# Linear-memory v and o columns as seven-product pairs ahead of attention, kept in DRAM until their heads

## The chip, the cores and the metric

The kernel runs on one core of one Trainium2 chip. Its time is that of one execution on the device in microseconds (us). A core has TensorE (PE) for matrix products, VectorE (DVE), ScalarE (ACT) and GpSimd (POOL) for the rest, and SyncE (SP), which here only issues DMAs. Each engine works through its own instructions in the order in which the program has them and waits on semaphores for the others. PE writes to PSUM, eight banks of 128 x 512 values; here four belong to a tag "mm" and four to a tag "aux".

## The reference

One inference step of a one-layer hybrid encoder on 512 frames of a new stream ("prompt") and 64 frames of a running one ("sample"), 576 rows in all, model width 1024:

```python
h = layer_norm(ALPHA * x + 0.5 * swiglu_ffn(x, ffn1_w_gu, ffn1_w_down), ln1_g, ln1_b)
z = h @ w_in      # q, k, v, o of 4 memory heads, gates i and f, q, k, v of attention, gates g_m and g_a
h_ml = mlstm(silu(conv(q)), silu(conv(k)) / 16, v, i, f, state)     # linear memory, chunks of 64
y_ml = (norm(h_ml) * ml_norm_g * sigmoid(o)) @ w_ml_proj
y_att = band_attention(qa, ka, va, cache, bias) @ w_att_proj
h = layer_norm(ALPHA * h + (sigmoid(g_m) * y_ml + sigmoid(g_a) * y_att) @ w_out, ln2_g, ln2_b)
y = layer_norm(ALPHA * h + 0.5 * swiglu_ffn(h, ffn2_w_gu, ffn2_w_down), ln3_g, ln3_b)
```

Outputs are y and the new states (convolution rows, memory C, n and m, keys and values). All is float32.

## The kernel before, in words

Activations lie transposed: a tile is 128 features by 576 rows, eight tiles make the width. Every product is computed as three products of rounded parts (float32r): value = hi + lo, and x w becomes hi hi, lo hi and hi lo (`mm3`, L127). **A column** is 128 output features: 8 feature blocks x 3 products x 2 halves of the rows (256 and 320) = 48 matmuls into two "mm" banks (`gemm`, L266). Its weights come as one DMA of 512 KB on SP; `pump` (L187) has ACT round them to hi, and lo is made either by DVE or (for most columns of `w_in`) by ACT, which writes -hi, and a DMA on POOL's queue that adds the raw weights to it (`add_lo`, L174). `plan` (L339 to L367) is the list of all weights in the order of use; `take` and `done` move along it.

**Seven-product pairs.** In both FFNs a gate column and an up column are computed together by a Strassen-like scheme: `Units` (L679) views the pair as a 2 x 2 block product over the two halves of the features and the two halves of the rows (288 each) and needs 7 instead of 8 block products: 7 x 4 feature blocks x 3 = 84 matmuls of 288 rows against 96 of a plain pair. The price is sums: of weights, per pair, on DVE and ACT (`prep`), and of activations, once, in `Combos` (L644): `add` makes 16 sums of halves on DVE, `make`, at high priority, has ACT round each of eight sums of 128 x 576 to hi and write -hi for lo (16 copies), and POOL issues eight DMAs that add the sum to lo. A pair's results are copied out of PSUM by ACT and combined on DVE.

**Stages**, in PE's order, with their starts in the profiled execution: FFN1 (0), the norm LN1 inside a wave of the first attention columns v, k, q and the memory gates "if" (401.5; `WAVE_M`, L1203: half 1 of v, k, q, half 1 of "if", then half 2 of them), attention for column pairs j = 0 to 7 (428.6), gate columns 64 to 71 (about 650), the attention projection "ap" (703), the four memory heads (755, 812.4, 881.6, 950.8), gate columns 56 to 63 (1020), the memory projection "mp" (1083.3), "o" (1134), LN2 and FFN2 (1187), LN3.

**A head** (L1324 to L1527) has eight columns: k, k, q, q, o, o, v, v. k and q go through a convolution (`conv_rest`), v is turned to rows (`turn5`) and split, o goes through a sigmoid and POOL multiplies it by the norm's gain. Between the columns stand the memory's own small products: `weights`, `state`, `hidden`, the norm, and `back`, which turns the normed rows back and multiplies by o.

**What sets the order.** PE's order is written by hand: `Order` (L42) has a modelled clock that every matmul moves on, `later(dt, fn)` puts a piece of work on a heap to be issued once the modelled clock reaches its due time, `od.bg` holds background work with a period, and `gemm` looks at both between matmuls. The other engines' orders are made by the framework's scheduler from issue order and priorities (`hot(n)`: that much higher). Buffers rotate in pools; an instruction that writes a buffer waits until its last reader is done.

In attention the sample rows' values (`values_s`, L1184) multiply probabilities with cached and new values: 2 heads x 3 key blocks (128, 128 and 64 keys) x 3 products, each 64 stationary columns (one head's width) by 64 rows.

Of the kernel before, what the change touches and what calls it, by code (L numbers as in the profile page):

```python
# [81 lines left out]
def tile_layer(ctx: ExitStack, tc: tile.TileContext, ins, outs):  # L82
# [10 lines left out]
    psum = ctx.enter_context(tc.tile_pool(name="psum", bufs=4, space=PSUM))  # L93

# [14 lines left out]
    def slot(dt, pool=None, tag="s", **kw):  # L109
        return (pool or slots).tile([P, T], dt, tag=tag, name=nm(tag), **kw)  # L110

# [54 lines left out]
    EARLY = [("gu2", j, e) for j in range(2) for e in range(2)]  # L166
    CP = (6, 7)
# [10 lines left out]
    def early(pool, key):  # L178
# [3 lines left out]
        hi, lo = parts[c] = tuple(pool.tile([P, 1024], F32R, tag=t, name=nm(t), bufs=len(EARLY)) for t in ("eh", "el"))  # L182
        act(hi, raw)
        add_lo(lo, hi, plan[c][1])

    @hot(30)
    def pump(limit=2):  # L187
        while True:
            c = wst["conv"]
            if wst["dma"] < len(plan) and plan[wst["dma"]][0] in EARLY:  # L190
                wst["dma"] += 1
                continue
            if c < len(plan) and plan[c][0] in EARLY:
                assert c in parts
                wst["conv"] += 1
                continue
# [45 lines left out]
    def done(c):  # L242
        del parts[c]
        wst["used"] -= plan[c][0] not in EARLY
        later(50, pump)
# [433 lines left out]
    class Units:  # L679
# [3 lines left out]
        def __init__(self, n, j0, hr, pool, wp, combos):  # L683
            self.w, self.hr, self.pool, self.wp, self.x = ins[f"w_gu{n}"], hr, pool, wp, combos
            self.raw, self.ws, self.p = {}, {}, {}
            self.js = list(range(j0, FT))

        def load(self, j):
            if j >= FT:
                return  # L690
            w = self.raw[j] = self.wp.tile([P, 2048], F32, tag="wu", name=nm("wu"), bufs=2)
            SP.dma_start(w[:, 0:1024], self.w[j])  # L692
            SP.dma_start(w[:, 1024:2048], self.w[FT + j])
# [11 lines left out]
        @hot(30)  # L705
        def prep(self, j, what):
            if j >= FT:
# [34 lines left out]
        def begin(self, j, tag="mm"):  # L742
            u = dict(j=j, X=bank(tag)[:, :HT_], h=self.hr.tile([P, T], F32, tag="h", name=nm("h"), bufs=FT + 1), tag=tag)
            self.product(u["X"], j, "a11", "b11", True, False)
            self.copy(u["h"][:, :HT_], u["X"])
            return u

        def second(self, u):
            h = u["h"][:, :HT_]
            Y = bank(u["tag"])[:, :HT_]  # L750
            self.product(Y, u["j"], "a12", "b21", True, True)
            with tc.high_priority(offset=60):
                tt(h, Y, h, ALU.add)
                act(h, h, AF.Silu)

        def run(self, tail):
            cur = ahead = None
            for j in self.js + [None]:
# [7 lines left out]
                if j == FT - 1:  # L766
# [10 lines left out]
                self.copy(new["h"][:, HT_:], new["X"])  # L777
# [4 lines left out]
                c = new["c"] = self.pool.tile([P, HT_], F32, tag="c22", name=nm("c22"), bufs=1)  # L782
# [4 lines left out]
                if j == FT - 1:  # L787
# [5 lines left out]
        def finish(self, u):  # L793
            j, h = u["j"], u["h"]
            self.product(u["X"], j, "a22", "t4", False, True)
            with tc.high_priority(offset=60):
                stt(h[:, :HT_], u["X"], -1.0, h[:, :HT_], ALU.mult, ALU.mult)
# [3 lines left out]
            with tc.high_priority(offset=60):  # L801
                tt(h[:, HT_:], u["Z"], h[:, HT_:], ALU.add)
                act(h[:, HT_:], h[:, HT_:], AF.Silu)
                last = tt(h[:, HT_:], h[:, HT_:], u["c"], ALU.mult)
            self.hr_done(j, h, last)
# [26 lines left out]
    def ffn(xs, n, gi, raw, final=None, prev=None):  # L832
        hh = {}
        with tc.tile_pool(name=nm("hr"), bufs=FT, side="right", reuse_waits="tile") as hr, \
# [30 lines left out]
            with tc.tile_pool(name=nm("sw"), bufs=1, side="right", reuse_waits="tile") as sw, \  # L865
                    tc.tile_pool(name=nm("sx"), bufs=1, side="right", reuse_waits="tile") as sx:
                combos.pool = sx
                un = Units(n, CL[n], hr, sx, sw, combos)
# [35 lines left out]
            with tc.tile_pool(name=nm("h1"), bufs=n1, side="right", reuse_waits="tile") as h1, \  # L904
# [3 lines left out]
                ln = Norm(xs, 2.0 * ALPHA, 4.0 * EPS, gi, final)  # L908
# [189 lines left out]
    def att_core(j, st):  # L1098
# [103 lines left out]

    gemm([[(("in", 48), KT)], [(("in", 40), KT)], [(("in", 32), KT)], [("if", KT)]], H,  # L1203
         [out_cb(vf0, "v", 0), out_cb(kf0, "k", 0), lambda hf, ps: act(hs(qf0, hf), ps), gate_cb], WAVE_M)
    ln1.close()
    opool.append(ostack.enter_context(tc.tile_pool(name="op", bufs=8, reuse_waits="tile")))
# [39 lines left out]
    matt = sg  # L1246
    for j in range(KT):
        gemm(one(("ap", j)), OS,
             [lambda hf, ps, m=matt[j]: tt(hs(m, hf), hs(m, hf), ps, ALU.mult)])
# [5 lines left out]
    sgp = gstack.enter_context(tc.tile_pool(name="sg0", bufs=2, side="right", reuse_waits="tile"))  # L1255
# [36 lines left out]
    def conv_rest(R, ct, scale, tail=None):  # L1292
# [7 lines left out]
        hi, lo = slot(F32R, mp, "qk", bufs=8), slot(F32R, mp, "qk", bufs=8)  # L1300
# [23 lines left out]
    def ml_qkov(h, early):  # L1324

        st = {"k": [], "q": [], "og": []}
# [3 lines left out]
        for e in range(2):  # L1330
# [3 lines left out]
            kf, hi, lo = conv_rest(R, ct, 1.0 / 16)  # L1334
# [9 lines left out]
            later(10000, lambda kf=kf, s=k_sink: turn5(kf, s))  # L1344
        qtail = mp.tile([P, 2, NS], F32, tag="qtail", name=nm("qtail"))
        for e in range(2):
# [3 lines left out]
            _, hi, lo = conv_rest(R, ct, 1.0, qtail[:, e, :])  # L1350
            st["q"].append((hi, lo))
        st["qtail"] = qtail
        early(st)
        for e in range(2):
            o = slot(F32, hp, "og")
            st["og"].append(o)
            gemm(one(("in", 24 + 2 * h + e)), H, [lambda hf, ps, o=o: act(hs(o, hf), ps, AF.Sigmoid)])
            ts(o, o, ccol(C_NG + 2 * h + e), 0.0, ALU.mult, ALU.add, eng=POOL)
        for e in range(2):
            vf = slot(F32, mp, "qf", bufs=2)  # L1360
            gemm(one(("in", 16 + 2 * h + e)), H, [lambda hf, ps, vf=vf: act(hs(vf, hf), ps)])
# [6 lines left out]
            later(2500, lambda vf=vf, s=v_sink: turn5(vf, s))  # L1368
        return st

    def ml_early(h, st):

        st["W"] = W = []
# [53 lines left out]
        for b in range(5):  # L1427
            later(15440 + 3120 * b, lambda b=b: weights(b))

    def ml_late(h, st):  # L1430
# [59 lines left out]
        def back(e):  # L1490
# [5 lines left out]
            og = st["og"][e]  # L1496
            tt(og[:, :NP_], pt, og[:, :NP_], ALU.mult)
            tt(og[:, NP_:], pt2[:, :NS], og[:, NP_:], ALU.mult)
# [7 lines left out]
        t = 4500  # L1506
        for e in range(2):
            later(t, lambda e=e: state(e))
            t += 1800
        for b in range(5):  # L1510
            later(t, lambda b=b: hidden(b))
            t += 1700
        later(t + 2500, norm)

    for h in range(4):
        st = ml_qkov(h, lambda st, h=h: ml_early(h, st))
        ml_late(h, st)
# [3 lines left out]
    for j in range(2):  # L1521
        s = sg[j] = slot(F32, sgp, "sg")
        gemm(one(("in", 56 + j)), H, [lambda hf, ps, s=s: act(hs(s, hf), ps, AF.Sigmoid)])
    od.drain()
# [6 lines left out]
    gmp = hts.enter_context(tc.tile_pool(name="gm", bufs=6, reuse_waits="tile"))  # L1531
# [10 lines left out]
    for j in range(2, KT):  # L1542
        s = sg[j] = slot(F32, gmp, "sg")
        gemm(one(("in", 56 + j)), H, [lambda hf, ps, s=s: act(hs(s, hf), ps, AF.Sigmoid)])
# [23 lines left out]
    for i, key in enumerate(EARLY):  # L1568
        later(4000 + 6800 * i, lambda key=key: early(epool, key))
# [96 lines left out]
```

## Time and profile before

| | us |
|---|---|
| median of three executions | 1597.05 (1596.64 to 1605.06) |
| the profiled execution | 1601.19 |
| its span, first to last instruction | 1599.4 |
| PE busy | 1580.9 |
| DVE busy | 990.2 |
| ACT busy | 875.1 |
| POOL busy | 199.9 |

The span is what the trace covers; 1.8 us of the profiled execution lie outside it. Times in a row of the profile count from the span's start. In a row of a timeline stand start, length, engine, line, operation, what is written and read, shapes and count, and in brackets how long the engine idled before it and which instruction ended that. L123 is the line of the helper that issues matmuls, L133 that of transposes, L137 of ACT's copies, L140, L143 and L147 of DVE's and POOL's operations, so rows are told apart by the tiles they name. PE's ends are modelled, so where paces are needed differences of starts are used.

### The profile page before, as it was taken

The numbers are of one execution on the slowest core, as the hardware profiler recorded it, in microseconds if no ns is written. First come the engines' busy times: TensorE is split into PE (matmuls) and PEld (weight loads), VectorE is DVE, ScalarE is ACT, GpSimd is POOL, SyncE is SP. The second block draws the span as 40 slices with busy tenths as digits, with TensorE's granted clock in tenths as the row PEclk, the third lists the DMA queues.
The fourth block names the chain that finished last, engine by engine and source line by source line (L and its number), as shares of the span: only waits on it lengthen the run. The fifth ranks groups of instructions, "written<-read, shape, count | busy, mean of one in ns | idle before, by whom it ended". The sixth has DMA issues, their size and how long they took to land. (4 is left out here: it accounts for less than half of the span.)

```text
span 1599.4 us, 29416 instructions
## 1 busy us (share of the span) xinstructions
PE 1580.9 (99%) x11851; PEld 1559.0 (97%) x11851; DVE 990.2 (62%) x2041; ACT 875.1 (55%) x1587; POOL 199.9 (12%) x363
## 2 busy tenths in 40 slices
PE   9999999999999999999999999999999999999998
PEld 8999999999999999999999999999999999999997
DVE  7777777636777677551545637234686777776636
ACT  7554556314677677863758576642446455555223
POOL 2000000000424334011212111102111000000000
PEclk9999999999999999999999999999999999999999
DMA  9222222224466666577656564642435232213333
GB/s 264 95 105 81 106 80 74 83 86 130 135 163 154 154 148 151 113 168 169 145 138 137 127 149 104 156 109 83 129 106 139 80 106 81 105 54 97 112 94 121
DMA packets 65921, 193.18 MB, mean 121 GB/s; under 512 B 7288, under 2 KB 17144, under 8 KB 65784
## 3 DMA queue, kind: packets, MB, share of 16 engines
q1 hardware_dynamic: 51672, 145.16, 27.3%
q0 software_dynamic: 13536, 45.62, 16.9%
q8 instruction: 93, 1.52, 0.4%
q10 hardware_dynamic: 576, 0.52, 0.1%
q14 instruction: 44, 0.36, 0.1%
HBM read 177.31 MB, written 9.24 MB: 117 GB/s over the span
## 5 line engine op out<-in xcount | busy, mean ns | idle before, releaser
L123 PE MATMUL mm<-s,wh 128*128 128x288 f32 (+2 forms) x3856 | 786.6, 298 | 0.9 <-ACT h L137 0.4
L123 PEld LDWEIGHTS mm<-s,wh 128*128 128x128 f32 x3856 | 618.8, 189 | 5.5 <-ACT s L418 0.9
L123 PE MATMUL mm<-s,wl 128*128 128x288 f32 (+2 forms) x1912 | 565.0, 295 | 0.8 <-DVE wl L140 0.7
L123 PEld LDWEIGHTS mm<-s,wl 128*128 128x128 f32 x1912 | 360.8, 189 | 1.2 <-DVE wl L140 1.2
L137 ACT ACTIVATE wh<-wr 128x1024 fp32r<-128x1024 f32 (+2 forms) x163 | 164.9, 1014 | 272.6 <-PE mm L123 246.4
L140 DVE TENSOR_TENSOR wl<-wr,wh 128x1024 fp32r<-128x1024 f32 (+2 forms) x88 | 101.2, 1157 | 128.0 <-ACT wh L137 127.8
L123 PE MATMUL mm<-h,wh 128*128 128x256 f32 (+1 forms) x672 | 134.7, 294 | 0.0
L140 DVE TENSOR_TENSOR wl<-ws,wh 128x1024 fp32r<-128x1024 f32 x39 | 47.8, 1225 | 104.0 <-ACT wh L137 103.8
L123 PEld LDWEIGHTS mm<-h,wh 128*128 128x128 f32 x672 | 107.6, 188 | 0.2
L123 PE MATMUL mm<-h,wl 128*128 128x256 f32 (+1 forms) x336 | 98.7, 294 | 0.0
L441 POOL TENSOR_TENSOR rs<-var,mhalf 128x2 f32<-128x2 f32 (+1 forms) x6 | 5.2, 863 | 740.2 <-DVE var L143 384.0
L137 ACT ACTIVATE wh<-ws 128x1024 fp32r<-128x1024 f32 x39 | 41.4, 1061 | 94.8 <-PE mm L123 94.3
L123 PE MATMUL mm<-tx,wh 128*128 128x288 f32 x448 | 92.4, 298 | 0.0
L176 POOL DMA_DIRECT2D wl<-in_w_in x66 | 57.9, 878 | 244.6 <-ACT wl L137 176.2
L137 ACT ACTIVATE wl<-wh 128x1024 fp32r<-128x1024 f32 x74 | 78.0, 1054 | 0.5
L123 PEld LDWEIGHTS mm<-tx,wh 128*128 128x128 f32 x448 | 72.1, 189 | 0.0
L123 PE MATMUL mm<-tx,wl 128*128 128x288 f32 x224 | 66.1, 295 | 0.0
L123 PEld LDWEIGHTS mm<-h,wl 128*128 128x128 f32 x336 | 63.0, 188 | 0.0
L123 PE MATMUL mm<-tx,ah 128*128 128x288 f32 x296 | 62.2, 302 | 0.1
L137 ACT ACTIVATE wh<-wu 128x1024 fp32r<-128x1024 f32 x39 | 41.4, 1062 | 30.6 <-PE mm L123 30.0
L123 PE MATMUL mm<-hb,wh 128*128 128x256 f32 (+1 forms) x280 | 56.5, 294 | 0.0
L123 PE MATMUL mm<-hc,wh 128*128 128x256 f32 (+1 forms) x280 | 56.3, 294 | 0.0
(322 smaller groups left out, 3294.0 us busy)
## 6 DMA issues: line engine op xcount, KB each, us to landing
wu<-in_w_gu SPq DMA_DIRECT2D x78, 512.0 KB, 4.3
wr<-in_w_in SPq DMA_DIRECT2D x72, 512.0 KB, 3.7
wl<-in_w_in POOLq DMA_DIRECT2D x66, 512.0 KB, 5.5
wr<-in_w_dn SPq DMA_DIRECT2D x40, 512.0 KB, 3.5
wr<-in_w_dn SPq DMA_DIRECT2D x20, 384.0 KB, 3.1
G<-in_rbias SPq DMA_DIRECT2D x16, 256.0 KB, 2.7
wr<-in_w_ap SPq DMA_DIRECT2D x8, 512.0 KB, 3.7
wl<-in_w_ap POOLq DMA_DIRECT2D x8, 512.0 KB, 6.1
```

Source lines behind the costliest of these rows:

```text
L123: PE.matmul(out, lhsT, rhs, start=start, stop=stop, **kw)
L137: ACT.activation(out, in_, func, **kw)
L140: return (eng or DVE).tensor_tensor(out, a, b, op=op)
L176: POOL.dma_start(lo, src, accum_op=ALU.add)
L441: return y, POOL.tensor_tensor(y, v, mhalf[:, :n], op=ALU.pow)
```

## The change

1. Columns 16 to 31 (v and o of the four heads) leave the heads. The first v pair (16, 17) is computed plainly behind LN1's wave, with weights loaded early; the other seven pairs, o0, v1, o1, v2, o2, v3, o3, follow as seven-product pairs (`Columns`, a second kind of `Units`), all ahead of attention. The sums of LN1's output come from `Combos`, so LN1 keeps its unsplit output as LN2 did (sixteen more ACT copies).
2. Their results (o after its sigmoid) are stored to DRAM, sixteen tiles of 128 x 576, and loaded again in their head. The gated attention output (eight tiles) is stored behind "ap" and loaded again ahead of "mp".
3. A head computes k, k, q, q and one gate column (56 + h). The norm's gain moves from POOL into the last product of `back`. Due times of the head's pieces change: weights at 11000 + 2600 b (15440 + 3120 b before), state at 5500, hidden at 19500 + 2200 b, the norm at 31000. Gate columns 60 to 62 follow the heads, and column 63 stands alone beside the eight splits of the heads' output (`ht_split`), which stood beside six gate columns.
4. `values_s` takes hi and lo of the values side by side as 128 stationary columns: 12 matmuls instead of 18, and one more ACT copy and two small DVE additions in place of two ACT copies.

In the core of the diff, `Units` takes its sources and its last steps from the subclass (`GateUp` holds the FFN's); that part is left out here.

```diff
@@ plan
     plan.append(("if", ins["w_if"]))
+    plan_in((16, 17))
+    stops.append(len(plan))
     for j in range(1, KT):
         plan_in((48 + j, 40 + j, 32 + j))
     plan_in(range(64, 72))
     plan += [(("ap", j), ins["w_ap"][j]) for j in range(KT)]
     for h in range(4):
-        plan_in((8 + 2 * h, 9 + 2 * h, 2 * h, 2 * h + 1, 24 + 2 * h, 25 + 2 * h, 16 + 2 * h, 17 + 2 * h))
-    plan_in(range(56, 64))
+        plan_in((8 + 2 * h, 9 + 2 * h, 2 * h, 2 * h + 1, 56 + h))
+    plan_in(range(60, 64))
@@ new class
+    class Columns(Units):
+        def __init__(self, pairs, sinks, out, pool, wp, combos):
+            super().__init__([(w_in[a], w_in[b]) for a, b in pairs], 0, pool, wp, combos)
+            self.sinks, self.out = sinks, out
...
+        def done21(self, u):
+            act(u["21"], u["X"], scale=-1.0)
+        def done(self, u):
+            self.sinks[u["j"]](u["o"])
@@ values_s
+            blocks = (P, 5), (P, 6), (NS, 4)
             for e in range(2):
                 r = slice(64 * e, 64 * e + 64)
-                for b, (ks, vb) in enumerate(((P, 5), (P, 6), (NS, 4))):
-                    mm3(po[0:64, r], vc[:ks, vb, e, 0:64], vc[:ks, vb, e, 64:128], th[:ks, b, r], tl[:ks, b, r],
-                        b == 0, b == 2)
+                for b, (ks, vb) in enumerate(blocks):
+                    for x in (th, tl):
+                        mm(po[:, r], vc[:ks, vb, e, :], x[:ks, b, r], b == 0 and x is th, b == 2 and x is tl)
+            tmp = ap_.tile([P, P], F32, tag="ts", name=nm("ts"))[0:64, :]
+            act(tmp, po[64:128, 0:P])
             for e in range(2):
-                act(o_[64 * e:64 * e + 64, NP_:T], po[0:64, 64 * e:64 * e + 64])
+                r = slice(64 * e, 64 * e + 64)
+                tt(o_[r, NP_:T], po[0:64, r], tmp[:, r], ALU.add)
@@ behind the first norm
+    combos = Combos(H, ln1.d, [slot(F32, stp, "st", bufs=8) for _ in range(8)])
+    for i, key in enumerate(EARLY1):
+        later(9000 + 4000 * i, lambda key=key: early(e1, key, EARLY1))
     gemm([[(("in", 48), KT)], [(("in", 40), KT)], [(("in", 32), KT)], [("if", KT)]], H,
          [out_cb(vf0, "v", 0), out_cb(kf0, "k", 0), lambda hf, ps: act(hs(qf0, hf), ps), gate_cb], WAVE_M)
+    VD, OD = [away("vd") for _ in range(KT)], [away("od") for _ in range(KT)]
+    for i in range(4):
+        combos.last = combos.add(i)
     ln1.close()
+    with tc.tile_pool(name="cx", bufs=1, side="right", reuse_waits="tile") as cx:
+        combos.pool = cx
...
+        un.load(0)
+        un.load(1)
+        combos.make()
+        un.prep(0, "a")
+        for c in range(2):
+            t = slot(F32, stp, "st", bufs=8)
+            def v_cb(hf, ps, t=t, c=c):
+                act(hs(t, hf), ps)
+                if hf == 1:
+                    SP.dma_start(VD[c], t)
+            gemm(one(("in", 16 + c)), H, [v_cb])
+            if c == 0:
+                with tc.issue_after(combos.last.ins):
+                    un.prep(0, "s")
+                un.prep(0, "t")
...
+        un.run(tail)
@@ heads
+        for e in range(2):
+            v = slot(F32, mp, "vf", bufs=2)
+            SP.dma_start(v, VD[2 * h + e])
+            st["v"].append(v)
+            SP.dma_start(st["og"][e], OD[2 * h + e])
...
-            later(15440 + 3120 * b, lambda b=b: weights(b))
+            later(11000 + 2600 * b, lambda b=b: weights(b))
...
-            tt(og[:, :NP_], pt, og[:, :NP_], ALU.mult)
-            tt(og[:, NP_:], pt2[:, :NS], og[:, NP_:], ALU.mult)
+            stt(og[:, :NP_], pt, g, og[:, :NP_], ALU.mult, ALU.mult)
+            stt(og[:, NP_:], pt2[:, :NS], g, og[:, NP_:], ALU.mult, ALU.mult)
...
+    for h in range(4):
+        st = ml_kq(h)
+        ml_early(h, st)
+        ml_late(h, st)
+        gate(h, sgp, "sg")
+    for j in range(4, 7):
+        gate(j, None, "s")
...
+    matt = [slot(F32) if j < 4 else slot(F32, gmp, "gm") for j in range(KT)]
+    for m, d in zip(matt, MD):
+        SP.dma_start(m, d)
+    gate(7, None, "s")
     od.force(lambda: len(HT.p) == KT)
```

More of the change, by code (lines that the diff above doesn't have):

```diff
@@ L243, in done @@
         del parts[c]
-        wst["used"] -= plan[c][0] not in EARLY
+        wst["used"] -= plan[c][0] not in EARLY + EARLY1
         later(50, pump)
@@ L706, in prep @@
         def prep(self, j, what):
-            if j >= FT:
+            if j >= self.end:
                 return
@@ L742, in begin @@
         def begin(self, j, tag="mm"):
-            u = dict(j=j, X=bank(tag)[:, :HT_], h=self.hr.tile([P, T], F32, tag="h", name=nm("h"), bufs=FT + 1), tag=tag)
+            u = dict(j=j, X=bank(tag)[:, :HT_], tag=tag)
+            self.outputs(u)
             self.product(u["X"], j, "a11", "b11", True, False)
-            self.copy(u["h"][:, :HT_], u["X"])
+            self.copy(u["11"], u["X"])
             return u
         def second(self, u):
-            h = u["h"][:, :HT_]
             Y = bank(u["tag"])[:, :HT_]
@@ L765, in run @@
                     return
-                if j == FT - 1:
+                if j == self.end - 1:
                     tail()
@@ L776, in run @@
                 self.product(new["X"], j, "s2", "t2", False, False)
-                self.copy(new["h"][:, HT_:], new["X"])
+                self.copy(new["12"], new["X"])
                 self.prep(j + 1, "t")
@@ L781, in run @@
                 self.product(new["X"], j, "s3", "t3", False, False)
-                c = new["c"] = self.pool.tile([P, HT_], F32, tag="c22", name=nm("c22"), bufs=1)
+                self.third(new)
+                c = new["22"]
                 self.copy(c, new["X"])
@@ L801, in finish, with __init__, outputs, third @@
             with tc.high_priority(offset=60):
[L802 to L805, printed above, removed]
+                tt(u["12"], u["Z"], u["12"], ALU.add)
+                self.done(u)
+    class GateUp(Units):
+        def __init__(self, n, j0, hr, pool, wp, combos):
+            w = ins[f"w_gu{n}"]
+            super().__init__([(w[j], w[FT + j]) for j in range(FT)], j0, pool, wp, combos)
+            self.hr = hr
+        def outputs(self, u):
+            h = u["h"] = self.hr.tile([P, T], F32, tag="h", name=nm("h"), bufs=FT + 1)
+            u["11"], u["12"] = h[:, :HT_], h[:, HT_:]
+        def third(self, u):
+            u["22"] = self.pool.tile([P, HT_], F32, tag="c22", name=nm("c22"), bufs=1)
+        def done11(self, u):
+            act(u["11"], u["11"], AF.Silu)
+        def done21(self, u):
+            stt(u["11"], u["X"], -1.0, u["11"], ALU.mult, ALU.mult)
+        def done(self, u):
+            act(u["12"], u["12"], AF.Silu)
+            self.hr_done(u["j"], u["h"], tt(u["12"], u["12"], u["22"], ALU.mult))
+    class Columns(Units):
+        def __init__(self, pairs, sinks, out, pool, wp, combos):
+            super().__init__([(w_in[a], w_in[b]) for a, b in pairs], 0, pool, wp, combos)
+            self.sinks, self.out = sinks, out
+        def outputs(self, u):
+            u["o"] = [slot(F32, self.out, "st", bufs=8) for _ in range(2)]
+            for e, o in enumerate(u["o"]):
+                u[f"{e + 1}1"], u[f"{e + 1}2"] = o[:, :HT_], o[:, HT_:]
+        def third(self, u):
+            pass
+        def done11(self, u):
+            pass
+        def done21(self, u):
+            act(u["21"], u["X"], scale=-1.0)
+        def done(self, u):
+            self.sinks[u["j"]](u["o"])
     class Hidden(Act):
@@ L1245, in tile_layer, with ap_cb, cb @@
     od.force(lambda: osq)
-    matt = sg
+    MD = [away("md") for _ in range(KT)]
+    def ap_cb(j):
+        def cb(hf, ps):
+            m = hs(sg[j], hf)
+            tt(m, m, ps, ALU.mult)
+            if hf == 1:
+                SP.dma_start(MD[j], sg[j])
+                sg[j] = None
+        return cb
     for j in range(KT):
-        gemm(one(("ap", j)), OS,
-             [lambda hf, ps, m=matt[j]: tt(hs(m, hf), hs(m, hf), ps, ALU.mult)])
+        gemm(one(("ap", j)), OS, [ap_cb(j)])
     ostack.close()
     od.force(lambda: gdone)
-    sgp = gstack.enter_context(tc.tile_pool(name="sg0", bufs=2, side="right", reuse_waits="tile"))
+    sgp = gstack.enter_context(tc.tile_pool(name="sg0", bufs=4, side="right", reuse_waits="tile"))
     hstack = ExitStack()
@@ L1322, in turn5, with ml_kq @@
             sink(b0, nb, w, ps[:w, :nb * P].rearrange("p (b c) -> p b c", c=P))
-    def ml_qkov(h, early):
-        st = {"k": [], "q": [], "og": []}
+    def ml_kq(h):
+        st = {"k": [], "q": [], "og": [slot(F32, hp, "og") for _ in range(2)], "v": []}
         kwh = mp.tile([P, 5, 256], F32R, tag="kwh", name=nm("kwh"))
@@ L1349, in ml_qkov, with ml_early @@
             gemm(one(("in", ct)), H, [cb])
-            _, hi, lo = conv_rest(R, ct, 1.0, qtail[:, e, :])
+            _, hi, lo = conv_rest(R, ct, 1.0, lambda: slot(F32R, mp, "qk", bufs=4), qtail[:, e, :])
             st["q"].append((hi, lo))
         st["qtail"] = qtail
[L1353 to L1361, printed above, removed]
+        return st
+    def ml_early(h, st):
+        st["W"] = W = []
+        for e, vf in enumerate(st["v"]):
             ce = slice(e * P, (e + 1) * P)
@@ L1505, in ml_late, with gate @@
         later(0, start)
-        t = 4500
         for e in range(2):
-            later(t, lambda e=e: state(e))
-            t += 1800
+            later(5500 + 1800 * e, lambda e=e: state(e))
         for b in range(5):
[L1511 to L1517, printed above, removed]
+            later(19500 + 2200 * b, lambda b=b: hidden(b))
+        later(31000, norm)
     mg = Act()
     sg = {}
-    for j in range(2):
-        s = sg[j] = slot(F32, sgp, "sg")
+    def gate(j, pool, tag):
+        s = sg[j] = slot(F32, pool, tag)
         gemm(one(("in", 56 + j)), H, [lambda hf, ps, s=s: act(hs(s, hf), ps, AF.Sigmoid)])
+    for h in range(4):
[3 more added lines that the diff above has]
+        gate(h, sgp, "sg")
+    del st
+    for j in range(4, 7):
+        gate(j, None, "s")
     od.drain()
```

85 lines of the change are left out of this document (54 added, 31 removed).

## The prediction

> **What bounds the kernel now.** I read the page first (engine shares, releasers), then the waits of TensorE (PE), then windows of the stages that the change touches, then the timelines around the end of the first norm.
>
> ```profile
> span 1599.4 us, 29416 instructions
> PE 1580.9 (99%) x11851; PEld 1559.0 (97%) x11851; DVE 990.2 (62%) x2041; ACT 875.1 (55%) x1587; POOL 199.9 (12%) x363
> ```
> PE is busy for 99% of the span, the other engines for 62% at most. A modelled busy time is not proof, so the waits come next (columns: what waited, for whom, us in total, times, longest):
>
> ```profile
> PE aux L123 <- DVE wl L140: 3.2, 2, 2.0
> PE mm L123 <- ACT h L137: 0.4, 1, 0.4
> ```
> The first row is the longest of all; the whole list adds up to under 10 us of 1599. So the time is PE's instruction stream, and an edit pays by the matmuls that it removes and costs by the PE idle time that it makes. The price of one matmul stands in the chain of work that ended last:
>
> ```profile
> 1234.73 2.56 PE aux L123 x10
> ...
> 1265.08 181.82 PE mm L123 x1362
> ```
> In the long stretch 1362 matmuls take 181.82 us: **0.133 us each** (the other row is used below). Now the stages: start:end and length, then busy us (instructions) of PE, PEld, DVE, ACT, POOL, the granted clock, the DMA share, GB/s.
>
> ```profile
> 166.90:178.10 11.20, 11.20 (x87) 11.18 (x85) 8.27 (x12) 5.67 (x9) 0.00 (x0) 1.00 0.28 95
> 409.90:415.00 5.10, 5.10 (x42) 4.94 (x42) 4.27 (x10) 1.78 (x6) 4.78 (x10) 1.00 0.23 78
> 428.60:448.00 19.40, 17.26 (x127) 15.96 (x127) 15.76 (x56) 17.63 (x39) 3.84 (x4) 1.00 0.83 230
> 510.70:580.00 69.30, 69.18 (x543) 67.39 (x542) 49.16 (x154) 50.88 (x118) 27.06 (x49) 1.00 0.64 156
> 881.60:950.80 69.20, 69.20 (x517) 67.23 (x516) 36.49 (x91) 47.15 (x89) 12.91 (x31) 1.00 0.57 134
> 1232.40:1234.70 2.30, 0.36 (x3) 0.13 (x1) 2.30 (x5) 0.00 (x0) 0.00 (x0) 1.00 0.72 290
> 1234.70:1240.00 5.30, 5.27 (x28) 5.27 (x29) 2.17 (x3) 2.21 (x4) 0.00 (x0) 0.68 0.01 2
> ```
> In order: one seven-product pair in FFN1; POOL's preparation for the first attention column, under the wave; the entry to attention; steady attention; the third head; the stall at FFN2's first unit; and the 5.3 us behind that stall.
>
> **The change, part by part.**
>
> 1. *Fewer matmuls.* A plain column is 48 matmuls, so a pair is 96 and a seven-product pair is 84. Seven of the eight v and o pairs change: 7 x 12 = 84 matmuls less. The removed and added products average 288 columns both ways, so the price is 0.133 us: **-11.2 us**. It counts in full, as a head has no idle PE to give back: 69.20 of 69.20 us busy.
>
> 2. *Sample values.* Per column pair of attention, 18 matmuls with 64 stationary columns become 12 with 128. Before's block, start, us and count of each row:
>
> ```profile
> 515.14 0.22 PE L123 MATMUL aux<-psl,vc 128*64 128x64 f32 x1
> 515.20 0.28 PE L123 MATMUL aux<-psh,vc 128*64 128x64 f32 x2
> ...
> 515.37 0.39 PE L123 MATMUL aux<-psh,vc 128*64 128x64 f32 x2
> 515.61 0.22 PE L123 MATMUL aux<-psl,vc 64*64 64x64 f32 x1
> ...
> 516.57 0.66 PE L133 MATMUL aux<-ident,sc 128*128 128x128 f32 x4
> 516.98 0.48 PE L123 MATMUL mm<-s,wh 128*128 128x256 f32 x2
> ```
> The block runs from 515.11 to 516.57, 1.46 us. One matmul takes 515.20 - 515.14 = 0.06 us; two with the change to 64 rows behind them take 515.61 - 515.37 = 0.24, so a change costs about 0.10, and the block has four. No row has 128 stationary and 64 moving columns. From below it is 0.06, from above the four 128x128 transposes, 0.41/4 = 0.10. A block is then 12 x 0.06 + 0.4 = 1.1 or 12 x 0.10 + 0.4 = 1.6, with eight blocks -2.9 to +1.1 us. I take the upper end, since the stationary size is the transposes': **+1**. The Trainium skill, TensorE: Matmul & The Clock Gate, "LDWEIGHTS (loading the stationary operand)", says that a load's time goes with its columns, rows not mattering: 53 ns for 64 and 107 ns for 128 by its formula. The trace's 0.06 agrees with the first; by the page the block's loads alone would grow from 0.96 to 1.28 us, 2.6 us in eight blocks, against this edit.
>
> 3. *Entry to the new stage.* PE goes from the wave's last half ("if", up to 428.60) to column 16, whose first matmul needs the PSUM bank of v's second half. In the changed program ACT has fifteen of the sixteen 128x576 copies of the sums ahead of that eviction, and ACT works in order. Before's ACT and DVE there, and the same copies and sums in FFN1:
>
> ```profile
> 20.51 0.67 ACT L137 ACTIVATE tx<-h 128x576 fp32r<-128x576 f32 x1
> ...
> 22.38 0.67 ACT L137 ACTIVATE tx<-h 128x576 fp32r<-128x576 f32 x1
> 22.95 0.67 ACT L137 ACTIVATE s<-s 128x576 fp32r<-128x576 f32 x1
> ```
> ```profile
> 419.96 1.48 ACT L137 ACTIVATE s<-s,cols 128x320 fp32r<-128x320 f32 x3 [1.23 <-DVE s L143]
> 425.40 2.01 ACT L137 ACTIVATE wh<-wr 128x1024 fp32r<-128x1024 f32 x2 [3.96 <-PE mm L123]
> 427.43 0.44 ACT L137 ACTIVATE vf<-mm 128x320 f32<-128x320 f32 x1
> ```
> ```profile
> 16.79 0.45 DVE L140 TENSOR_TENSOR h<-s 128x288 f32<-128x288 f32 x1
> 17.16 0.45 DVE L140 TENSOR_TENSOR h<-s,s 128x288 f32<-128x288 f32 x1
> ```
> ```profile
> 420.76 1.47 DVE L143 SCALAR_TENSOR_TENSOR s<-s,cols,s 128x320 fp32r<-128x320 f32 x3
> ```
> The norm's last operation on DVE ends at 422.2. The sums take 0.37 to 0.4 us each, two make a tile's first copy possible, so ACT starts copying near 423. At 22.95 - 22.38 = 0.57 us a copy fifteen take 8.6 us, to 431.6; a little more where ACT waits for DVE early on, and 0.44 for the eviction: PE goes on at about 432.4 instead of 428.6, **+3.8 us** (1 if half the copies fit in earlier gaps, 6 if the sums start late). The mechanism is in before at a smaller size:
>
> ```profile
> 26.52 0.50 PE L123 MATMUL mm<-s,wh 128*128 128x256 f32 x2 [0.42 <-ACT h L137]
> ```
> There PE waited 0.42 us for a bank behind such copies. A stall costs more than itself: after the idle 2 us ahead of 1234.70 the clock is 0.68 over 5.3 us, and ten matmuls take 2.56 us instead of 1.33; 28 in 5.30 us instead of 3.73. **+1.6** (0 to 2). The Trainium skill, same page, Part 1 "What's actually happening", says that the gate halves the clock after an idle window of some 3.4 us and needs as long to reopen; the half rate agrees with 0.256 us per matmul, while the stall here was shorter than that window.
>
> 4. *Leaving the stage.* POOL's preparation of the first attention column (4.78 busy of 5.10 us, hidden under the wave) and its loads now queue behind the last unit: POOL's come after the weight DMA of the next column, SP's after the unit's stores. Columns of the next pair run meanwhile, but the scores can't. If all is hidden it costs 0; if none is, 5. Entry to attention already lost 19.40 - 17.26 = 2.1 us in before, part of which it replaces. I take **+2**.
>
> 5. *Heads.* Each loses three columns, 3 x 48 x 0.133 = 19.2 us: 69.2 becomes 50.0 us. ACT's groups in the third head (count, then busy us, mean ns, idle before and its releasers):
>
> ```profile
> L137 ACT ACTIVATE wh<-wr 128x1024 fp32r<-128x1024 f32 x8 | 8.5, 1064 | 3.5 <-PE mm L123 3.5
> L137 ACT ACTIVATE wl<-wh 128x1024 fp32r<-128x1024 f32 x8 | 8.4, 1054 | 0.0
> ...
> L137 ACT ACTIVATE kwh<-aux,tcol 128x128 fp32r<-128x128 f32 x8 | 2.9, 361 | 4.2 <-DVE kwl L143 3.5 <-PE aux L133 0.6
> ...
> L137 ACT ACTIVATE qk<-qf 128x576 fp32r<-128x576 f32 x4 | 2.7, 685 | 1.4 <-DVE qf L143 1.3
> ...
> L137 ACT ACTIVATE hf<-aux 128x258 f32<-128x258 f32 x4 | 1.5, 387 | 4.1 <-PE aux L123 4.1
> L137 ACT ACTIVATE vh<-aux 128x512 fp32r<-128x512 f32 x2 | 1.2, 600 | 1.7 <-PE aux L133 1.7
> ...
> L137 ACT ACTIVATE og<-mm 128x320 f32<-128x320 f32 x2 | 0.8, 424 | 0.0
> ...
> L137 ACT ACTIVATE cn<-aux 128x258 f32<-128x258 f32 x2 | 0.8, 387 | 4.1 <-PE aux L123 2.2 <-DMA out_pC<-cn 1.9
> ```
> Three of eight weight pairs go, 3/8 of 16.9 = 6.3 us, and of the evictions of four columns, two halves each at some 0.4 us, one column's stay: 2.4 us. ACT has about 38.4 of 50.0 us, 77%, and DVE 36.5, 73%. Steady attention runs at 73% and 71% and PE idles 0.12 us of 69.30. So the heads stay PE's, a little tighter: **+1.5** for four, 0 if the slack holds. The chain per head (weights, state, hidden, norm) has its due times set shorter; the eight splits of the heads' output now stand beside one gate column of 6.4 us instead of six: **+0.5**.
>
> 6. *Moved or free.* A DMA of the same size, issued on SP (count, KB each, us to landing):
>
> ```profile
> out_v<-s SPq DMA_DIRECT2D x7, 288.0 KB, 4.0
> ```
> 48 DMAs of 288 KB on SP add 14 MB. The DMA share in a head is 0.57 and v and o are asked for two columns before use, 12 us: nothing; were the cover gone, one landing of 4.0 us per head. The gain moved from POOL into the last product, and sixteen more copies in the norm: nothing outside step 3.
>
> **The sum.** -11.2 + 1 + 3.8 + 1.6 + 2 + 1.5 + 0.5 = -0.8 us. The profiled execution took 1601.19 us (span 1599.4 and 1.8 outside), so it would be 1600.4; the median of the runs shown is 1597.05, 4.1 lower, so the forecast there is **1596.3 us**.
>
> **Rivals.**
>
> *A, the gain comes through.* ACT's copies fit into the gaps (ACT idles from 421.4 to 425.4 in before) and the attention entry is covered: steps 3 to 5 shrink from 9.4 to between 1 and 3 us. With step 2 at +1 that is 1597.05 - 11.2 + 1 + 1 to 3 = 1588 to 1590, with step 2 at its lower end 1584: 1588 as the likeliest. For it: PE's share in all other stages. Against: the written order of ACT.
>
> *B, the heads become ACT's.* This ends slower. ACT works in order, and its waits for the head's own chain in the rows above are 4.2 + 1.4 + 4.1 + 1.7 + 4.1 = 15.5 us per head. If they do not shrink with the head, a head takes 38.4 + 15.5 = 53.9 us instead of 50.0, four heads 15.6 us more, and the sum with step 5's 1.5 replaced is +13.3: **1610 us**. It decides from 50.0 - 38.4 = 11.6 us of such waits on. For it: chain and due times were spread over 69 us. Against: many waits are ACT being early, as PE never waited.
>
> *C, the two ends of the new stage cost more:* sums late (6), clock (2), attention entry (5): +13 instead of 7.4, 1602.
>
> *D, the change doesn't do what it says.* Were the units' weight sums on DVE (8.27 of 11.20 us in FFN1) to bind, seven units would lose their 11.2 us: 1607.5. Against: FFN1's pair has PE busy 11.20 of 11.20.
>
> **How the numbers follow.** A measurement of this kernel tells about 0.5%, 8 us, from no change, so "same" is 1589 to 1605. Forecast with C: 0.46, nearly all same. A: 0.27, nearly all faster. B and D: 0.27, slower. Low is A with step 2 between its ends, 1586, and high is B with 2 us of C, 1612; about 1 in 10 lies beyond each. Faster 0.27, same 0.45, slower 0.28.
>
> **What would show it.** Step 1: a head window near 50 us and a unit of 11.2 us. Step 2: the block of sample values at 1.1 or 1.6 us. Step 3: a wait of PE "mm" for ACT of 3 to 4 us right behind the wave, with a clock under 1.00 for some 5 us after it; none would make A right. Step 4: PE idle beyond 2.1 us around the first scores. Step 5: PE's busy share in the heads; under 97% would make B right. A wait of PE for a DMA of v, o or the gated attention would make step 6 wrong.

## The result and the profile after

The changed kernel takes 1607.91 us (median of 7 runs, 1606.72 to 1613.35), the kernel before 1599.95 us (7 runs): a ratio of **1.0057, 95% interval 1.0038 to 1.0077**, 8 us or some 0.5% slower. The forecast was 0.8 us faster. It started from the 1597.05 us of three executions of the kernel before; seven gave 1599.95, so 2.9 of the 11.6 us between the forecast 1596.3 and the result come from that median. The profiled execution of each kernel agrees: a span of 1606.1 us against 1599.4.

The head of the page of after:

```profile
span 1606.1 us, 29438 instructions
PE 1576.4 (98%) x11719; PEld 1554.9 (97%) x11719; DVE 1051.4 (65%) x2143; ACT 897.6 (56%) x1624; POOL 188.0 (12%) x349
```

PE has 132 matmuls fewer, 84 of the seven pairs and 8 x 6 of the sample values, so the products did go. It is busy 4.5 us less, and yet the span is 6.7 us longer: span less busy time is 29.7 us where before had 18.5. The waits of PE in after (what waited, for whom, us in total, times, longest):

```profile
PE mm L128 <- ACT vf L142: 3.7, 1, 3.7
PE aux L138 <- DVE vl L145: 3.2, 3, 1.1
...
PE aux L138 <- ACT s L142: 2.7, 1, 2.7
PE aux L128 <- DVE kl L1127: 1.4, 1, 1.4
...
PE aux L128 <- POOL kh L152: 1.2, 1, 1.2
PE aux L138 <- ACT Mb L142: 1.0, 1, 1.0
```

Of these six only `s` stands in before's list, with 0.4 us. They belong to three places: the first row to the entry to the new stage, `s`, `kl` and `kh` to the entry to attention, `vl` and `Mb` to the heads (one wait in each of the four). Windows of after (start:end and length, then busy us and instructions of PE, PEld, DVE, ACT, POOL, the granted clock, the DMA share, GB/s):

```profile
429.60:433.28 3.68, 0.00 (x0) 0.00 (x1) 1.35 (x3) 3.65 (x8) 2.85 (x4) 1.00 1.06 180
433.28:437.04 3.76, 3.76 (x18) 3.76 (x19) 1.61 (x2) 3.71 (x9) 1.25 (x2) 0.55 1.08 197
446.10:525.85 79.75, 79.75 (x601) 79.67 (x600) 46.94 (x61) 40.97 (x63) 0.00 (x0) 1.00 0.34 113
525.85:545.25 19.40, 13.62 (x97) 12.79 (x96) 12.12 (x36) 13.76 (x27) 10.32 (x22) 0.94 0.68 192
542.30:549.60 7.30, 6.79 (x34) 6.52 (x34) 5.71 (x26) 4.63 (x14) 1.07 (x2) 0.53 0.77 184
941.40:992.62 51.22, 50.17 (x374) 47.89 (x373) 36.43 (x92) 38.54 (x79) 9.20 (x26) 1.00 0.56 131
1243.20:1248.50 5.30, 5.30 (x41) 5.30 (x42) 2.02 (x3) 2.10 (x4) 0.00 (x0) 1.00 0.00 1
```

In order: PE idle 3.68 us ahead of column 16; the 3.76 us behind it at a clock of 0.55; the seven-product stage, 601 matmuls in 79.75 us with no idle time; the same 19.40 us of the attention entry that the prediction showed of before, with 13.62 us busy instead of 17.26; 7.30 us at a clock of 0.53; one head, 51.22 us from one wait to the next instead of 69.2; and the 5.30 us behind a wait of 1.9 us at FFN2's first unit, at full clock. The sample values in after (start, us, and count of each row):

```profile
558.51 0.30 PE L128 MATMUL aux<-psh,vc 128*128 128x64 f32 x1 [0.40 <-DVE ptl L145]
558.65 0.28 PE L128 MATMUL aux<-psl,vc 128*128 128x64 f32 x1
558.76 0.28 PE L128 MATMUL aux<-psh,vc 128*128 128x64 f32 x1
558.87 0.28 PE L128 MATMUL aux<-psl,vc 128*128 128x64 f32 x1
559.08 0.29 PE L128 MATMUL aux<-psh,vc 64*128 64x64 f32 x1
...
560.31 0.66 PE L138 MATMUL aux<-ident,sc 128*128 128x128 f32 x4
```
```profile
588.92 0.20 PE L128 MATMUL aux<-psh,vc 128*128 128x64 f32 x1
...
590.62 0.55 PE L138 MATMUL aux<-ident,sc 128*128 128x128 f32 x3
```

The first block of twelve runs from 558.51 to 560.31, 1.80 us; the second, from 588.92 to 590.62, takes 1.70, as do the five behind it (the eighth takes 1.78). Eighteen took 1.46 in most of before's blocks. Over the eight blocks, without the waits inside them, that is 13.8 us instead of 11.8.

### The profile page after: what moved, and what is told of

Same layout as the page of the kernel before. It is cut to its first block, busy times and chain, and to the rows that moved or that the text cites. A ratio compares the mean times of both kernels' runs of the same rounds, so it can differ in the third digit from the quotient of the medians.

```text
span 1606.1 us, 29438 instructions
## 1 busy us (share of the span) xinstructions
PE 1576.4 (98%) x11719; PEld 1554.9 (97%) x11719; DVE 1051.4 (65%) x2143; ACT 897.6 (56%) x1624; POOL 188.0 (12%) x349
## 5 line engine op out<-in xcount | busy, mean ns | idle before, releaser
L128 PE MATMUL mm<-s,wh 128*128 128x288 f32 (+2 forms) x3574 | 732.6, 299 | 0.2 <-ACT s L427 0.2
L128 PEld LDWEIGHTS mm<-s,wh 128*128 128x128 f32 x3574 | 576.3, 190 | 3.7 <-issue 0.6
L128 PE MATMUL mm<-s,wl 128*128 128x288 f32 (+2 forms) x1771 | 524.9, 296 | 0.7 <-DVE wl L145 0.7
L128 PEld LDWEIGHTS mm<-s,wl 128*128 128x128 f32 x1771 | 335.8, 190 | 1.0 <-DVE wl L145 1.0
L142 ACT ACTIVATE wh<-wr 128x1024 fp32r<-128x1024 f32 (+2 forms) x147 | 148.1, 1009 | 247.1 <-PE mm L128 224.5
L128 PE MATMUL mm<-tx,wh 128*128 128x288 f32 x522 | 106.9, 296 | 0.0
L182 POOL DMA_DIRECT2D wl<-in_w_in x50 | 45.0, 900 | 280.7 <-ACT wl L142 246.7
L142 ACT ACTIVATE wl<-wh 128x1024 fp32r<-128x1024 f32 x58 | 61.2, 1055 | 0.5
L145 DVE TENSOR_TENSOR ws<-wu 128x1024 f32<-128x1024 f32 x46 | 56.0, 1218 | 7.1 <-DMA wu<-in_w_gu 6.9
L145 DVE TENSOR_TENSOR wl<-wt,wh 128x1024 fp32r<-128x1024 f32 x46 | 56.0, 1218 | 6.5 <-ACT wh L142 6.5
```

The costliest lines, as they stand in the source:

```text
L128: PE.matmul(out, lhsT, rhs, start=start, stop=stop, **kw)
L142: ACT.activation(out, in_, func, **kw)
L145: return (eng or DVE).tensor_tensor(out, a, b, op=op)
L182: POOL.dma_start(lo, src, accum_op=ALU.add)
```

## The experiments

The theory after the result: the product saving is whole, and it is more than spent by four separate, local losses. Each of the first four runs takes one of them away from the changed kernel. The intervals of the ratios are 1.5 to 3 us wide on either side, so what a run takes off the changed kernel is known to some 4 us. The rival was that one loss stands for another (an engine too full at that place), so that the wait moves instead of going.

**1. Evictions first.** The rounding of the sums loses its raised priority:

```diff
-        @hot(80)
-        def make(self):
+        def make_plain(self):
...
+        make = hot(80)(make_plain)
...
-        combos.make()
+        combos.make_plain()
```

> The sixteen copies of the sums lose their raised priority, so that ACT evicts the wave's second halves (v, k, q) before most of them; nothing else is changed. Theory (four separate waits): the 3.7 us wait of PE for ACT's eviction behind the wave and the slow clock after it go, 3.9 + 1.6 = 5.5 us off the changed kernel's span of 1606.1, to about 1600.6; the waits at the first scores and in the heads stay as they are. Rival (the work in front of the first unit is too much for ACT and DVE, whatever its order): the stall moves to the first unit, PE then waits there for weights or for the sums, and the span stays within 2 us of 1606.

Measured: 1600.15 us, ratio to before 1.0008 [0.9995, 1.0021], span 1598.6. By the ratios 7.8 us are gone, which their intervals don't tell from the 5.5 expected. PE's row for ACT `vf` has left the list, and the stretch has no idle time and a full clock. ACT's timeline in this run shows the new order, and the window behind it that PE does not wait:

```profile
425.12 0.67 ACT L142 ACTIVATE tx<-tx 128x576 fp32r<-128x576 f32 x1
425.81 0.44 ACT L142 ACTIVATE vf<-mm 128x320 f32<-128x320 f32 x1
426.14 0.43 ACT L142 ACTIVATE kf<-mm 128x320 f32<-128x320 f32 x1
```
```profile
425.00:446.00 21.00, 21.00 (x158) 21.00 (x157) 14.03 (x20) 16.53 (x31) 6.27 (x8) 1.00 0.94 220
```

In after the same eviction stood behind fifteen copies:

```profile
431.53 0.67 ACT L142 ACTIVATE tx<-tx 128x576 fp32r<-128x576 f32 x1
432.10 0.67 ACT L142 ACTIVATE s<-st 128x576 fp32r<-128x576 f32 x1
432.79 0.44 ACT L142 ACTIVATE vf<-mm 128x320 f32<-128x320 f32 x1
```

No stall came up at the first unit, so the rival falls at this place: it was the order of ACT's work, not its amount. The waits at the first scores did not stay as they were, though: PE's wait for `s` fell from 2.7 to 1.0 us. Behind the waits for `kh` and `kl` (1.2 and 1.4 us, as in after) PE ran at 0.50 from 528.69 to 532.10, where after had a full clock, and so came to the next wait later.

**2. First bias tile early.** Only `G` of attention column 0 and its mask move ahead of the units:

```diff
+        G0 = [slot(F32)[:, :512] for _ in range(2)]
+        for e in range(2):
+            SP.dma_start(G0[e], ins["rbias"][e])
+            POOL.memset(G0[e][0:64, 448:512], NEG)
...
+            if j == 0:
+                st["G"] = G0
+                return
```

> The bias tile G of the first attention column and its mask on GpSimd are made ahead of the units (in two free slots), and only that is moved; keys and values are still prepared behind the units. Theory: VectorE's first score operation waits 2.8 us for the mask, which stands in GpSimd's queue behind the loads of cached keys and values; without that wait PE's 2.7 us wait for ACT and the half clock behind it (some 3 us) go, and the two waits for kh and kl (1.2 and 1.4 us) stay: about 5 us off, 1601. Rival (the entry is bound by the rounding of keys, not by the mask): under 1.5 us off, and PE idles as long at the same place.

Measured: 1603.0 us, ratio 1.0024 [1.0010, 1.0039], 5.3 us off by the ratios. The row "PE aux L138 <- ACT s" is gone. What after had at the place, in POOL's and DVE's timelines (start, us, what, and in brackets the idle time before it and what ended it):

```profile
534.05 0.56 POOL L152 TENSOR_SCALAR vc<-vp 128x128 fp32r<-128x128 f32 x2 [2.09 <-DMA vp<-in_vpast]
...
538.66 0.15 POOL L1080 MEMSET G<- 64x64 f32 x1
```
```profile
538.84 0.29 DVE L1177 CUSTOM_DVE_ANT_0 sc<-aux,G 128x128 f32<-128x128 f32 x1 [2.77 <-POOL G L1080]
```

The mask, 0.15 us of work, stood in POOL's queue behind the rounding of the cached values and keys, 4.6 us that it does not need and that had itself waited 2.09 us for a load; the first score operation waited for the mask. How this reaches PE stands in after's timelines of ACT and PE:

```profile
539.59 0.40 ACT L142 ACTIVATE sc<-sc,mx 128x128 f32<-128x128 f32 x1 [0.82 <-DVE mx L152]
540.63 0.51 ACT L142 ACTIVATE sc<-sc,mx 128x256 f32<-128x256 f32 x1 [0.55 <-DVE mx L152]
541.29 0.61 ACT L142 ACTIVATE sc<-sc,mx 128x384 f32<-128x384 f32 x1
541.90 0.41 ACT L142 ACTIVATE s<-mm 128x320 f32<-128x320 f32 x1
```
```profile
542.37 0.56 PE L138 MATMUL aux<-ident,s 128*128 128x128 f32 x3 [2.71 <-ACT s L142]
```

ACT's exponentials (`sc`) wait for the scores' maxima (`mx`), and behind them in ACT's order stands the eviction (`s`) of the second half of the next column pair's v. PE waits 2.71 us for that eviction, with the transposes of that v, and not for the scores. The waits for `kl` and the key copy stay, and so does a slow stretch behind them:

```profile
PE aux L128 <- DVE kl L1131: 2.0, 1, 2.0
...
PE aux L128 <- ACT kh L142: 1.2, 1, 1.2
```
```profile
533.30:536.90 3.60, 3.60 (x17) 3.60 (x16) 2.32 (x10) 1.10 (x4) 2.96 (x6) 0.53 0.77 207
```

**3. Old sample values.** The diff is the hunk `values_s` of the change, taken back.

> The sample values alone go back to 18 matmuls of 64 stationary columns; the rest is the changed kernel. Theory: each of eight blocks takes 1.46 us instead of 1.80, 2.7 us off: about 1603.4. Rival (the blocks run beside a wait that ends no earlier): no change.

Measured: 1605.71 us, ratio 1.0047 [1.0032, 1.0062], 1.6 us off by the ratios, 2.2 by the medians; not to be told from the changed kernel by itself. Its blocks take 1.46 us again, 2.0 us less over the eight. Run 11, below, asks the same of the kernel before.

**4. Second v tile later.** 

```diff
-            later(1000 + 1300 * e, lambda vf=vf, s=v_sink: turn5(vf, s))
+            later(1000 + 3900 * e, lambda vf=vf, s=v_sink: turn5(vf, s))
```

> In a head the second v tile is turned 3.9 us (modelled) behind the first instead of 1.3. Theory: PE's wait of 1.1 to 1.2 us in each head for a PSUM bank that VectorE has not yet emptied goes, four times: 4.5 us off, about 1601.5. Rival (VectorE is behind by the convolution of the last q, whatever the spacing): the wait stays or moves to the next transposes, under 1.5 us off.

Measured: 1631.32 us, ratio 1.0202 [1.0186, 1.0219], 23 us **slower** than the changed kernel: both expectations missed. The bank wait went in three of the four heads, and a worse one came:

```profile
PE aux L128 <- ACT vh L142: 12.3, 4, 3.6
```
```profile
947.30:1006.80 59.50, 55.58 (x373) 52.58 (x373) 36.15 (x92) 38.96 (x78) 9.07 (x26) 0.89 0.47 112
951.30:963.00 11.70, 7.78 (x31) 6.54 (x31) 4.24 (x10) 7.88 (x14) 1.12 (x4) 0.60 0.51 129
```

The state's products, due at 5.5 us, need both v tiles turned. PE met them too early in all four heads, by up to 3.6 us, and over the 11.7 us of the second window, that idle time included, the clock is 0.60 on average: a head of 59.5 us.

**5. State moved too.** The step between the v tiles is 2.6 us, and the state is due at 7.5 us instead of 5.5:

```diff
-            later(1000 + 1300 * e, lambda vf=vf, s=v_sink: turn5(vf, s))
+            later(1000 + 2600 * e, lambda vf=vf, s=v_sink: turn5(vf, s))
...
-            later(5500 + 1800 * e, lambda e=e: state(e))
+            later(7500 + 1800 * e, lambda e=e: state(e))
```

> In each head the second v tile is turned 2.6 us behind the first (1.3 in the changed kernel, 3.9 in the run that lost 24 us) and the state's products are due at 7.5 instead of 5.5 us. Theory: the 24 us came from the state's products meeting v tiles that were not turned yet; with the state moved too, PE's wait of 1.2 us per head for a PSUM bank goes, up to 4.8 us off, about 1603.5. Rival (v's turn and the state stand on ACT's path through the head, so that later is always worse): slower than 1608.

Measured: 1605.20 us where before had 1601.45 in the same runs, ratio 1.0030 [1.0018, 1.0042], 4.3 us off by the ratios. Of the four waits of a microsecond the first head's is left, and a head has PE busy throughout:

```profile
938.00:989.20 51.20, 51.20 (x382) 48.86 (x381) 36.84 (x96) 37.05 (x81) 9.01 (x26) 1.00 0.55 131
```

So what the heads lost came from their due times.

**6. First scores later, alone.** 

```diff
-        t = 4500
+        t = 4500 if j else 10500
```

> The changed kernel with only the first scores' due time moved from 4.5 to 10.5 us (modelled). Theory (PE meets the first scores too early, and nothing else is wrong at that place): the waits of 1.2, 1.4 and 2.7 us and the half clock go, up to 8 us off, about 1600. Rival (the preparation is on the path of the whole attention stage, so that every later piece shifts with it): the same idle time shows at a later place, under 2 us off.

Measured: 1608.09 us, ratio 1.0046 [1.0029, 1.0062], within 2 us of the changed kernel. The waits for `kh`, `kl` and `s` are gone from the list, and another stands there:

```profile
PE aux L138 <- DVE psl L145: 2.6, 1, 2.6
```

The theory's 8 us did not come, but the rival is not shown either. At the place itself its trace has one wait of 2.6 us instead of three of 5.3 in all, and 3.4 us of half clock behind it instead of 6.8, some 4 us less. The execution lost most of that again elsewhere: it ran at 0.50 from 1184.62 to 1188.03 and from 1242.65 to 1246.06, ahead of FFN2 and at its first unit, which the edit does not touch and where after had a full clock. With four executions the ratio can't tell the rival's 2 us from the trace's 4.

**7 to 9. Together.** Evictions first, bias early and old values:

> The changed kernel with the evictions first, the first bias tile early and the old sample values together. Theory (the losses are separate and add up): 7.8 + 4.9 + 2.2 us measured alone give 14.9 off 1607.9, 1593.0, 0.4% under the kernel before. Rival (with one wait gone, the next one behind it takes over): 1597 or more, no faster than before.

Measured: 1598.12 us, ratio 0.9984 [0.9975, 0.9994]. The three had taken off 0.0049, 0.0033 and 0.0010 alone, which would give 0.9965; 3 us of that did not come. That sum has the uncertainty of three runs and, twice over, of the changed kernel, some 7 us, so the 3 us are not shown to be more than noise. In its trace PE still waits for the keys' copies at the first scores, longer than in after for `Mb` in the first head, and longer than in before for FFN2's first weights:

```profile
PE aux L128 <- DVE wl L145: 4.3, 2, 3.1
...
PE aux L138 <- ACT Mb L142: 2.3, 1, 2.3
PE aux L128 <- DVE kl L1130: 2.0, 1, 2.0
PE aux L128 <- ACT kh L142: 1.2, 1, 1.2
```

With the first scores 3 us later as well (`t = 4500 if j else 7500`):

> As the kernel with three undone, and the first attention column's scores are due 3 us (modelled) later, 7.5 instead of 4.5 us. Theory: what is left at the attention entry (1.2 us for kh, 1.4 us for kl) is PE reaching the scores ahead of the keys' rounding, so later scores let the columns of the second pair run in that time: 2.5 us less, about 1590.5. Rival (the delay runs into the second pair's preparation, which reuses the key buffers): a new wait of as much there, no gain or 1 to 3 us lost.

Measured: 1598.11 us, ratio 0.9980 [0.9967, 0.9993]: no difference that can be told. And the three with the heads' move:

> Evictions first, first bias tile early, old sample values and the head's state and v turn moved apart, all together. Theory (the four losses are separate): the run with three stood at 0.9984 of before, and the heads' move alone took 1.0057 to 1.0030, so 0.9957, about 1593 where before is 1600. Rival (the heads' waits only pass on a delay that ends elsewhere, as part of the three did): 0.998 as without it.

Measured: 1597.26 us, ratio 0.9975 [0.9964, 0.9985], nearer to the rival's 0.998, which its interval holds, than to the theory's 0.9957, which it does not.

**10. All of it.** The three, the heads' move and the first scores at 7.5 us:

> The same and the first scores due 3 us later, which alone on top of three made 0.9984 to 0.9980. Theory: 0.995, 1592. Rival: no difference to the run without the later scores.

Measured: 1595.62 us where before had 1599.85, **ratio 0.9971 [0.9960, 0.9983]**: the fastest here, 4.6 us under before and 13.8 under the changed kernel by the ratios. The theory's 0.995 lies outside the interval, and the run without the later scores, 0.9975, inside: that they help is not shown. What PE still waits for in it:

```profile
span 1594.6 us, 29514 instructions
PE 1570.3 (98%) x11767; PEld 1547.7 (97%) x11767; DVE 1046.4 (66%) x2127; ACT 888.0 (56%) x1624; POOL 186.5 (12%) x349
```
```profile
PE aux L128 <- DVE wl L145: 4.5, 2, 3.4
PE mm L128 <- ACT h L142: 2.1, 1, 2.1
PE aux L138 <- ACT Mb L142: 2.1, 1, 2.1
PE aux L138 <- DVE psl L145: 1.9, 1, 1.9
```

PE is busy 10.6 us less than in before, but its span less busy time is 24.3 us against 18.5. So more than half of the saving is still lost to waits.

**11. The kernel before with only the new sample values.** The hunk `values_s` put into the kernel before.

> The kernel before with only the sample values as 12 matmuls of 128 stationary columns. Theory (the new form is slower on PE, 1.80 us a block for 1.46): 2.7 us on top, 1.0017 of before. Rival (the taken-over value of the prediction, 1 us in all): 1.0006, not to be told from no change.

Measured: 1603.84 us, ratio 1.0015 [1.0004, 1.0026], 2.4 us: the new form is slower. Its blocks take 1.70 to 1.80 us, as in the changed kernel, so they show 2.0 us. The ratio by itself does not tell this from the prediction's 1 us (1.0006), and the 2.7 us expected came from the first block alone.

## Why the prediction was wrong, step by step

The direction came out wrong, though every place of the loss stood in the sum. The step that failed is **step 4**, "I take +2": it had the place right but not the path from the mask to PE nor the slow clock, and came out 5 us short. Steps 2 and 5 were mis-sized too, by 1 and 2 us.

1. *Fewer matmuls, -11.2 us: right.* 601 records in 79.75 us are 0.133 us each with no idle time, and a head's period fell from 69.2 to 51.22 us with 1.05 us of wait in it; without the waits PE is busy 51.20 of 51.20 us.
2. *Sample values, +1 us: too small.* A matmul with 128 stationary and 64 moving columns takes 0.11 us (558.76 to 558.87), and a change to 64 rows still adds 0.10 (558.87 to 559.08 is 0.21). Twelve make 1.70 us in most blocks; I had 0.10 each from the transposes. +2.0 by the blocks, and run 11's +2.4 agrees within its interval. The estimate by the Trainium skill beside my sum (TensorE: Matmul & The Clock Gate, "LDWEIGHTS (loading the stationary operand)"), +2.6 for the loads, was nearer than +1, and the trace's 0.11 us agrees with its 107 ns for 128 columns.
3. *Entry, +3.8 and +1.6: right in place, cause and size.* 3.68 us idle, then 18 matmuls in 3.76 us instead of 2.1 at 0.119 each: 5.3 us. Run 1 showed the cause, ACT's order, and gave back 7.8 us; what is above 5.3 is within the uncertainty, and in its trace 1.7 us of wait at the first scores had gone too.
4. *Attention entry, +2: some 7.* PE idles 5.8 us in the 19.4 us where before idled 2.1, 3.7 more; then it runs 7.30 us at a clock of 0.53, 3.4 us lost. I had named the queue of POOL and counted its busy time (5 us at the most), but I had not followed the mask: DVE's score operations wait for it, ACT's exponentials for DVE, and an eviction that PE needs stands behind the exponentials. And I had no slow clock at this place. Run 2 took the mask out and 5.3 us went; the waits for `kh` and `kl` and 3.4 us of half clock stayed.
5. *Heads, +1.5 and +0.5: 4.2.* ACT has 38.5 of 51.2 us and DVE 36.4, nearly what was worked out, and neither is full: rival B's mechanism did not come. The loss is 1.0 to 1.1 us in each head (3.2 for `vl` and 1.0 for `Mb`), where the last transpose of a v tile finds no free bank. I had weighed the density and not the new due times. Run 5 removed three of the four waits; run 4 showed how narrow the place is: 2.6 us further on, the state stands.
6. *Moved or free: right.* No wait of PE for a load of v, o or the gated attention appears.

The sum as measured: -11.2 + 2.0 + 5.3 + 7 + 4.2 = +7.3 us, between +6.7 by the spans and +8.0 by the medians. Two more slow stretches cancel between the two profiled executions: one in the wave of after (0.51 from 406.20 to 409.70, 1.00 at that place in run 1) and the one at FFN2's first unit of before, where after has a full clock. Of the rivals, C had the right place, with 5 us for the attention entry, and still came out at 1602. D's 1607.5 lies nearest to the measured time by luck: its mechanism did not come, as the new stage has no idle time.

What stays open is whether the repairs add up, since the missing 3 us are within the uncertainty, and why two other waits are longer with the old sample values. In the five traces of the changed kernel that have them, the longest wait at FFN2's first unit is 3.1 to 3.4 us and that for `Mb` 2.1 to 2.8; in the six with the new ones they are 1.5 to 1.9 and 1.0 to 1.3. In the kernel before it is the other way round at FFN2: 2.0 us with the old values and 3.4 with the new. No edit touches FFN2's code, and with one trace of each kernel the cause stays open.

## What to carry to other kernels

In a kernel whose one engine is 99% busy, a saving on that engine is certain to the matmul, and what eats it stands at the seams: list for each seam what the first instruction behind it needs, and follow each need through the in-order queues that make it, from engine to engine and however small the work (a mask of 0.15 us cost some 5 us, by way of DVE and ACT). Price a single stall at its length and, by these traces, at 0, 1.7 or 3.4 us of half clock on top. Where pieces have due times by hand, look on both sides of each: one that is moved away from a full buffer may run into the next one that needs its result.

## What was not expected of the hardware

- The length of a stall did not tell how much slow clock came behind it. After an idle 3.68 us PE ran at 0.55 for 3.76 us, a loss of 1.7 us. Behind the wait of 2.7 us for `s` it ran at 0.53 for 7.30 us in after, a loss of 3.4, and at 0.75 for 6.90 us (541.00 to 547.90) in run 5, a loss of 1.7. A wait of 2.0 us at FFN2's first unit was followed by 0.68 over 5.3 us in before, and one of 1.9 by a full clock in after; a wait of 2.8 us for `Mb` was followed by a full clock in run 3 (888.60 to 896.00). Such a difference between two executions is of the size of the repairs that were measured here.
- Twice as many stationary columns cost more than a third fewer matmuls saved: 18 with 64 columns took 1.46 us, 12 with 128 took 1.70, though the moving side has 64 in both.
